# Split input-projection weights kept in DRAM between the two halves of the tokens

## The chip, the cores and the metric

The kernel runs on one core of a Trainium2 chip. Five engines work on their own instruction streams, each in order: TensorE (PE in the profile, PEld for its weight loads), VectorE (DVE), ScalarE (ACT), GpSimd (POOL) and SyncE (SP), which here only issues transfers. A transfer can be issued by SP, ACT or POOL. Engines wait for each other through semaphores. The metric is device time in microseconds (us) for one launch, less is better.

## The reference

One layer of a hybrid decoder over 2048 prompt tokens and 8 x 8 sample tokens, model width 1024. A combined input projection feeds a convolution branch and an RWKV-7 branch; an output projection with a residual and a final norm follow.

```python
xn = rms_norm(x, norm_g)
p = xn @ w_in                                   # 1024 -> 4224 columns
h, bg, cg, gc = conv columns, 512 each
u = cg * h;  z = causal width-3 convolution of u;  y_conv = bg * z * silu(gc)
pr = pr + mu_shift * (pr_prev - pr)             # token shift of the other 2176 columns
r, k, v, wl, al, gr = pr columns
S = S * w_t + (S @ -kk_t) (kk_t * a_t)^T + v_t k_t^T;  o_t = S r_t     # per head, 64 x 64
y_rwkv = (group_norm(o) + (r . k . r_k) v) * silu(gr)
y = x + concat(y_conv, y_rwkv) @ w_out;  return rms_norm(y), states
```

All of it is float32, and the products of the input projection have to be close to float32 in accuracy.

## The kernel before

The tokens are worked in two halves (`hf` 0 and 1) of 1024, the sample tokens with the first. A half is cut into three blocks of 256 or 330, 384 and 384 columns (`half_blocks`). The normalised inputs of a half lie transposed in SBUF as two parts, `xh` (rounded to the float32r type that TensorE multiplies) and `xl` (the rest), made by `xprep`.

`w_in` has 33 tiles of 128 output columns. `project` (line 297) takes one or two tiles: `load_w` (line 288) brings a tile's weights into SBUF and splits them in the same way, then per block 24 matmuls run, for each of the 8 slices of the contraction `wh*xh`, `wh*xl` and `wl*xh`, into one of two PSUM banks `pj`, and a function given by the caller empties the bank. The tile's weights are loaded and split in each half again, so 66 times in all.

`load_w` works in two pieces of 256 KB: SP issues the load into `wr` (two buffers), ACT copies it with rounding into `wh`, POOL subtracts to get `wl` (`split`, line 205; the copy is line 117, the subtraction line 207). `wh` and `wl` have two buffers each, so the weights of a tile are written when the tile two before it is done.

Two half times four pairs of heads make eight rounds (line 915, `s` = 0 to 7). A round projects k, r, then v and the gate together (`rwkv_pair`), and block by block computes decays, `bk` (lines 516 and 523), the A matrices (`amat`, POOL's `AB` at line 539) and sends diagonal blocks to DRAM (`dn`, line 622). `inverse` loads them back as `na` (line 634), runs a forward substitution on DVE (`subst`: the pairs `sub`, `xi`), sends the result out as `dx` and back into `AB` (line 663). `wkv` runs the recurrence in chunks of 64 tokens. `conv_group` projects the four convolution tiles h, C, B and G of the round, with sums on POOL (line 351) and DVE products that empty `pj` (shown as `hp` at line 123). In round 3 the convolution comes before the inverse, and `xprep(1)` follows it. After round 7 come the weights of the output projection and its 17 tiles.

The code is written stage after stage, but a planner sets the order of each engine's instructions from estimated durations, so that in the trace projections of the convolution run beside the substitution, and projections of the next round beside the recurrence. Buffers and waits are set by the same framework.

Of the kernel before, what the change touches and what calls it, by code (L numbers as in the profile page):

```python
# [8 lines left out]
F32 = mybir.dt.float32  # L9
# [6 lines left out]
DRAM = bass.MemoryType.DRAM  # L16
# [4 lines left out]
KT = D // 128  # L21
# [66 lines left out]
def trunk_kernel(ctx, tc, I, O):  # L88
    nc = tc.nc
    act, dve, pe, pool, sync = nc.scalar, nc.vector, nc.tensor, nc.gpsimd, nc.sync  # L90
# [5 lines left out]
    dram = ctx.enter_context(tc.tile_pool(name="dram", bufs=1, space=DRAM))  # L96
    cnt = [0]

    def T(pool, shape, tag, bufs=1, dt=F32):
        cnt[0] += 1  # L100
        return pools[pool].tile(shape, dt, tag=tag, bufs=bufs, name=f"{tag}_{cnt[0]}")
# [28 lines left out]

    yd = [[dram.tile([D, bl.nt], F32, name=f"yd{hf}{bl.i}") for bl in half_blocks(hf)] for hf in range(2)]

    # constants and parameters
    cst = T("const", [128, NCONST], "cst")
    warm = T("small", [128, 1], "ss", 2)
    pool.memset(warm, 0.0)
# [46 lines left out]
    for p in range(NPAIR):  # L183
        t = T("const", [128, 64], f"sst{p}")
# [1 line left out]
        sst.append(t)  # L186

    def rsqrt(x, n, rows=128, tag="x"):
        """x <- 1/sqrt(x) on [rows, n] of positive floats."""
        w = {"g": 6, "n": 3, "x": 1}[tag]  # L190
        nb = 2
        y = T("small", [128, w], "nwy" + tag, nb)[:rows, :n]
        a = T("small", [128, w], "nwa" + tag, nb)[:rows, :n]
        dve.tensor_scalar(out=a.bitcast(I32), in0=x.bitcast(I32), scalar1=1, scalar2=None,
                          op0=ALU.logical_shift_right)
        dve.tensor_scalar(out=y.bitcast(I32), in0=a.bitcast(I32), scalar1=-1.0, scalar2=MAGIC,
                          op0=ALU.mult, op1=ALU.add)
        for _ in range(3):
            mul(a, y, y)
            stt(a, a, -0.5, x)  # L200
            stt(y, a, 1.5, y, ALU.add, ALU.mult)
        return y

    # normalised inputs, transposed and split
    def split(hi, lo, src, eng=dve):
        copy(hi, src)
        eng.tensor_tensor(out=lo, in0=src, in1=hi.bitcast(F32), op=ALU.subtract)  # L207
# [77 lines left out]
                act.dma_start(out=O["shift_p"], in_=xts[-1][127:128, :])  # L285
        return xh, xl

    def load_w(src):
        wh = T("w", [128, KT, 128], "wh", 2, F32R)
        wl = T("w", [128, KT, 128], "wl", 2, F32R)  # L290
        for q in range(2):
            wr = T("w", [128, 4, 128], "wr", 2)
            sync.dma_start(out=wr, in_=src[:, q * 4:q * 4 + 4, :])
            split(wh[:, q * 4:q * 4 + 4, :], wl[:, q * 4:q * 4 + 4, :], wr, pool)
        return wh, wl

    def project(xs, hf, *tiles):
        ws = [load_w(I["w_in"][col // 128]) for col, _ in tiles]
        for bl in half_blocks(hf):
            for (wh, wl), (_, evac) in zip(ws, tiles):  # L300
                xh, xl = xs[0][bl.i], xs[1][bl.i]
                ps = PS([128, bl.cols], "pj", 2)
                for k in range(KT):
                    mm(ps, wh[:, k, :], xh[:, k, :], start=(k == 0), stop=False)
                    mm(ps, wh[:, k, :], xl[:, k, :], start=False, stop=False)
                    mm(ps, wl[:, k, :], xh[:, k, :], start=False, stop=(k == KT - 1))
                evac(bl, ps)
                yield
# [4 lines left out]
    def s8(ap):  # L313
        return ap[:, 0:64].rearrange("p (b j) -> p b j", j=8)

    # convolution branch
    def conv_group(xs, hf, g):
        sp = 80 if hf == 0 else 0
        u = T("half", [128, 1108], "hp", 4)
# [56 lines left out]
        yield from project(xs, hf, (CW + g * 128, ev_b))  # L376
        yield from project(xs, hf, (3 * CW + g * 128, ev_g))

    # token shift
    def shifter(hf, i, dst):  # L380
        state = {}

# [32 lines left out]
    def rwkv_pair(S, xs, la):  # L415
        hf, p = S.hf, S.p
# [4 lines left out]
        k = T("half", [128, 1108], "hp", 4)  # L421
        rr = T("half", [128, 1108], "hp", 4)
        ws = tmp()[:, 0:256]
# [16 lines left out]
        W = {}  # L440
# [9 lines left out]
            W[bl.i] = (wp, ws)  # L450

        def parts(bl):
            """(token slice, inner length, chunk slice, W view) of the sample and prompt parts of a block."""
            r = []
            e = 0
            if bl.samp:
                r.append((0, SAMP, slice(0, 1), W[bl.i][1], 8))
                e = 1
            r.append((bl.o, bl.np, slice(e, e + bl.nch), W[bl.i][0], 64))
            return r  # L460
# [136 lines left out]
        yield from vg  # L597

    def subst(na, x, n, par):
        """x[c, t] (columns c of the inverse, par of them per row step) by forward substitution."""  # L600
        rows = na.shape[0]
        cw = x.shape[1]
        for s in range(n - 1):
            w = min(s // par + 1, cw)
            m = n - 1 - s
            t = T("small", [128, 144], "sub", 1)[:rows, :w * m].rearrange("p (c t) -> p c t", t=m)
            mul(t, x[:, 0:w, s:s + 1].to_broadcast([rows, w, m]),
                na[:, s, s + 1:n].unsqueeze(1).to_broadcast([rows, w, m]))
            tt(x[:, 0:w, s + 1:n], x[:, 0:w, s + 1:n], t, ALU.add)
            if s % 4 == 3:  # L610
                yield

    def store_blocks(S, bl):
        """the diagonal 32 x 32 blocks to DRAM, one 64-token unit after the other."""
        if bl.i == 0:
            cnt[0] += 1
            S.dn = dram.tile([2, 2, 16, 32, 32], F32, tag="dn", bufs=2, name=f"dn_{cnt[0]}")
        e = 1 if bl.samp else 0
        for h in range(2):
            for b in range(2):  # L620
                r = h * 64 + b * 32
                sync.dma_start(out=S.dn[h, b, bl.ch0:bl.ch0 + bl.nch].rearrange("c s t -> s c t"),
                               in_=S.AB[bl.i][r:r + 32, e:e + bl.nch, b * 32:b * 32 + 32])
# [54 lines left out]
            copy(AB[0:32, e:e + n, 32:64], pt[0:32])  # L678
            dve.tensor_copy(out=AB[64:96, e:e + n, 32:64], in_=pt[64:96])

    # recurrence
    def group_tiles(S, bi, ca, n):
        """token-major beta/k (rows as in L) and v of up to four chunks of a block."""
        bt = T("ch", [128, 4, 128], "bt", 2)
        sv = T("ch", [128, 4, 2, 64], "sv", 2)
        pb = CX([128, 4, 128])
        for i in range(n):
            pe.transpose(out=pb[:, i, :], in_=S.bk[bi][:, ca + i].rearrange("p a t -> p (a t)"), identity=ident)  # L688
        copy(bt[:, 0:n, :], pb[:, 0:n, :])
        o = ca * 64  # L690
        if n == 1:
            pv = CX([64, 128])
            pe.transpose(out=pv, in_=S.v[bi][:, o:o + 64], identity=ident)
            copy(sv[64:128, 0, 0, :], pv[:, 0:64])
            copy(sv[0:64, 0, 1, :], pv[:, 64:128])
        else:
            m = n // 2
            pv = CX([128, m, 128])
            for i in range(m):
                pe.transpose(out=pv[:, i, :], in_=S.v[bi][:, o + i * 128:o + i * 128 + 128], identity=ident)  # L700
            svv = sv.rearrange("p (i r) h v -> p i r h v", r=2)
            for par in range(2):
                rows = slice(par * 64, par * 64 + 64)
                copy(svv[64:128, 0:m, par, 0, :], pv[rows, :, 0:64])
                copy(svv[0:64, 0:m, par, 1, :], pv[rows, :, 64:128])
        return bt, sv
# [115 lines left out]
        sync.dma_start(out=O["wkv_s"][p], in_=s0)  # L822

    def gn_out(S, ob, bl):
        """group norm, bonus and gate of a block."""
        e = 1 if bl.samp else 0
        n = bl.nch + e
        BV, SG = S.bv[bl.i], S.sg[bl.i]
# [35 lines left out]
        stt(yo, yo, pcol(P_LB, p), SG[:, :n * 64], ALU.add, ALU.mult)  # L864
        sync.dma_start(out=yd[S.hf][bl.i][CW + p * 128:CW + (p + 1) * 128, :], in_=yo)

    # output projection
    def out_weights():
        woh, wol = [], []
        for i, (a, n) in enumerate(((0, 2), (2, 3), (5, 3))):  # L870
# [44 lines left out]
    for s in range(8):  # L915
        hf, p = divmod(s, NPAIR)
# [43 lines left out]


def layout(inputs):
    """the arrays of the launch: the inputs, laid out with features on the partitions where the chip wants them."""
    import numpy as np

    def cols(name):
        return np.asarray(inputs[name]).reshape(-1, 128).T

    a = {n: np.asarray(inputs[n]) for n in inputs}
    r = {  # L970
        "consts": constants()[0],
        "masks": constants()[1],
        "params": np.concatenate([cols(n) for n in ("mu_shift", "k_k", "k_a", "r_k", "lnx_g", "lnx_b", "w0", "a0",
                                                    "conv_w")], axis=1),
        "w_da": np.concatenate([np.tile(a[n][0].reshape(64, NPAIR, 128).transpose(1, 0, 2), (1, 2, 1))
                                for n in ("w_dec2", "w_a2")], axis=2),
        "state_conv": a["state_conv"].reshape(NB * 2, 4, 128).transpose(2, 1, 0),
        "state_shift": a["state_shift"].reshape(NB, KT, 128).transpose(2, 1, 0),
        "state_wkv": a["state_wkv"].reshape(NB, NPAIR, 2, HD, HD).transpose(1, 2, 4, 0, 3).reshape(
            NPAIR, 128, NB, HD),  # L980
        "w_in": a["w_in"].reshape(KT, 128, -1, 128).transpose(2, 1, 0, 3),
        "w_out": a["w_out"][0],
        "norm_g": a["norm_g"],
        "final_norm_g": a["final_norm_g"],
        "x_prompt": a["x_prompt"][0],
        "x_sample": a["x_sample"].reshape(SAMP, D),
    }
    return {n: np.ascontiguousarray(v) for n, v in r.items()}
# [22 lines left out]
```

## Time and profile before

| | us |
|---|---|
| median of 3 runs | 1674.99 (1674.01 to 1675.52) |
| profiled execution: span from first to last instruction | 1669.8 |
| PE busy | 1548.2 (93%) |
| PEld busy | 1293.2 (77%) |
| DVE busy | 1046.6 (63%) |
| ACT busy | 652.7 (39%) |
| POOL busy | 338.2 (20%) |
| ACT's 132 copies into `wh` | 80.2 |

The page gives no other time of the profiled execution than its span. A busy share of an engine is an average over stages; PE's is that of a pipeline whose ends are modelled. A line of a group gives the engine, the operation, what it writes and reads, the number of instructions, the busy time, the mean of one in ns, and the idle time of the engine just before them with what ended it. In the timeline the number in brackets is that idle time and its releaser. Line 123 is the helper of most DVE operations, line 129 that of all matmuls, so one goes by the names of the tiles.

### The profile page before, as it was taken

The page shows a single profiled execution, that of the slowest core. Times are in us where ns is not written, and L with a number is a line of the kernel's source. Part 1 is how long each engine was busy: PE and PEld are TensorE (multiplying, and loading weights), DVE is VectorE, ACT ScalarE, POOL GpSimd, SP SyncE. Part 2 cuts the span into 40 slices and gives each one's busy share as a digit, 9 for nine tenths or more (in the row PEclk, how much of TensorE's full clock was granted, in tenths as well). Part 3 has the DMA queues.
Part 4 walks back from the last instruction along what each step waited for, and adds up shares of the span by engine and source line. Part 5 has one row for each costly group of instructions (what it writes and reads, how often), then busy time and mean ns, then how long its engine had stood idle before and what let it go on. Part 6 is the DMA issues. An engine that isn't in the chain of part 4 may idle for free.

```text
span 1669.8 us, 29362 instructions
## 1 busy us (share of the span) xinstructions
PE 1548.2 (93%) x11088; PEld 1293.2 (77%) x11088; DVE 1046.6 (63%) x3101; ACT 652.7 (39%) x1657; POOL 338.2 (20%) x395
## 2 busy tenths in 40 slices
PE   4989999989989999879988998899989999899997
PEld 4979778887778778867778778877887788567885
DVE  6377557765776469775577457745774577566554
ACT  5333345324532455254442454245424542342221
POOL 3233112421032103321033112311231123100000
PEclk9989999899989999989989998999899989799999
DMA  5101201120012102331012101210121023523441
GB/s 170 50 28 44 62 30 31 44 67 29 21 47 56 47 23 60 92 96 37 22 34 63 46 23 35 63 46 23 34 63 46 23 59 92 155 77 124 139 145 51
DMA packets 112463, 99.99 MB, mean 60 GB/s; under 512 B 61561, under 2 KB 85625, under 8 KB 112322
## 3 DMA queue, kind: packets, MB, share of 16 engines
q1 hardware_dynamic: 107024, 87.23, 18.0%
q10 hardware_dynamic: 5266, 10.86, 1.8%
q8 instruction: 88, 1.44, 0.4%
q14 instruction: 53, 0.43, 0.1%
q0 software_dynamic: 32, 0.03, 0.0%
HBM read 75.30 MB, written 22.75 MB: 59 GB/s over the span
## 4 chain that ended last, share of the span: by engine, by line
PE 64%; DVE 22%; DMA 5%; issue 4%; ACT 3%; SPq 1%; POOL 1%; POOLq 0%; ACTq 0%; DVEq 0%
PE pj L129 42%; PE ca L129 5%; PE ax L129 5%; DVE sub L123 5%; DVE xi L123 4%; PE cb L129 4%; PE oo L129 2%; DVE hp L123 2%; PE cx L129 2%; DMA na<-dn 2%; DVE bk L123 1%; DVE t L120 1%; PE cx L688 1%; DVE hp L120 1%; PE ax L282 1%
## 5 line engine op out<-in xcount | busy, mean ns | idle before, releaser
L129 PE MATMUL pj<-xh,wh 128*128 128x384 f32 (+3 forms) x1856 | 660.5, 356 | 31.8 <-DVE hp L123 30.4
L129 PE MATMUL pj<-xh,wl 128*128 128x384 f32 (+3 forms) x1856 | 658.8, 355 | 0.0
L129 PE MATMUL pj<-xl,wh 128*128 128x384 f32 (+3 forms) x1856 | 656.3, 354 | 2.6 <-POOL xl L207 2.2
L129 PEld LDWEIGHTS pj<-xh,wh 128*128 128x128 f32 x1856 | 360.3, 194 | 69.4 <-DVE hp L123 28.3
L129 PEld LDWEIGHTS pj<-xl,wh 128*128 128x128 f32 x1856 | 361.1, 195 | 30.2 <-POOL xl L207 3.0
L129 PEld LDWEIGHTS pj<-xh,wl 128*128 128x128 f32 x1856 | 360.2, 194 | 27.2 <-issue 2.7
L207 POOL TENSOR_TENSOR wl<-wr,wh 128x512 fp32r<-128x512 f32 x132 | 173.4, 1328 | 459.0 <-ACT wh L117 321.4
L117 ACT ACTIVATE wh<-wr 128x512 fp32r<-128x512 f32 x132 | 80.2, 625 | 162.9 <-PE pj L129 119.1
L117 ACT ACTIVATE tS<-sv,wc 64x64 f32<-64x64 f32 x256 | 88.0, 344 | 130.2 <-DVE sv L120 104.3
L129 PE MATMUL ax<-L,bk 64*128 64x128 f32 x528 | 89.5, 325 | 35.7 <-DVE bk L123 25.8
L129 PEld LDWEIGHTS ax<-L,bk 64*128 64x128 f32 x528 | 74.0, 219 | 54.2 <-POOL wl L207 26.7
L120 DVE SCALAR_TENSOR_TENSOR sv<-cb,wc,tS 64x64 f32<-64x64 f32 x240 | 67.9, 283 | 63.5 <-PE cb L129 52.2
L123 DVE TENSOR_TENSOR sub<-xi,na 128x126 f32<-128x126 f32 (+22 forms) x248 | 91.1, 367 | 17.3 <-DMA na<-dn 10.0
L117 ACT ACTIVATE t<-pj,prm 128x384 f32<-128x384 f32 (+3 forms) x170 | 68.8, 433 | 62.7 <-PE pj L129 59.5
L516 POOL TENSOR_TENSOR bk<-t,t 64x384 f32<-64x384 f32 (+2 forms) x56 | 56.2, 1003 | 173.8 <-ACT t L488 91.4
L736 DVE TENSOR_SCALAR u<-ca,Q 128x64 f32<-128x64 f32 x128 | 36.2, 283 | 85.7 <-PE ca L129 85.4
L123 DVE TENSOR_TENSOR xi<-xi,sub 128x126 f32<-128x126 f32 (+22 forms) x248 | 83.0, 335 | 7.3
L129 PEld LDWEIGHTS ca<-sv,L 128*64 128x64 f32 x528 | 43.4, 136 | 38.6 <-DVE sv L120 12.2
L726 DVE COPY xs<-ca 128x64 f32<-128x64 f32 x128 | 28.7, 225 | 68.7 <-PE ca L129 58.5
L129 PE MATMUL ca<-sv,L 128*64 128x64 f32 x528 | 68.4, 247 | 0.0
L123 DVE TENSOR_TENSOR AB<-ax,msk 64x384 f32<-64x384 f32 (+2 forms) x88 | 48.6, 553 | 28.9 <-PE ax L129 27.9
L123 DVE TENSOR_TENSOR hp<-pj,hp 128x512 f32<-128x512 f32 (+1 forms) x34 | 23.4, 689 | 62.6 <-PE pj L129 61.7
(201 smaller groups left out, 2027.1 us busy)
## 6 DMA issues: line engine op xcount, KB each, us to landing
wr<-in_w_in SPq DMA_DIRECT2D x132, 256.0 KB, 2.7
hp<-in_x_prompt SPq DMA_DIRECT2D x29, 512.0 KB, 3.7
la<-yd SPq DMA_DIRECT2D x16, 512.0 KB, 3.9
out_y_p<-hp ACTq DMA_DIRECT2D x16, 512.0 KB, 2.7
na<-dn SPq DMA_DIRECT2D x16, 256.0 KB, 4.0
hp<-in_w_out SPq DMA_DIRECT2D x8, 512.0 KB, 4.1
yd<-hp SPq DMA_DIRECT2D x16, 192.0 KB, 1.9
yd<-c SPq DMA_DIRECT2D x16, 192.0 KB, 1.9
```

The lines of the kernel that those rows point to most:

```text
L117: act.activation(out=out, in_=in_, func=AF.Copy, scale=scale, bias=bias)
L120: eng.scalar_tensor_tensor(out=out, in0=in0, scalar=scalar, in1=in1, op0=op0, op1=op1)
L123: dve.tensor_tensor(out=out, in0=in0, in1=in1, op=op)
L129: pe.matmul(out, lhsT=lhsT, rhs=rhs, start=start, stop=stop)
L207: eng.tensor_tensor(out=lo, in0=src, in1=hi.bitcast(F32), op=ALU.subtract)
L282: pe.transpose(out=ps[:, k, :], in_=xt[:, kk * 128:(kk + 1) * 128], identity=ident)
L516: pool.tensor_tensor(out=S.bk[bl.i][hs, chs, h, :], in0=ta[hs, a:a + n].rearrange("p (c j) -> p c j", j=64), in1=wi[hs, a:a + n].rearrange ...
L688: pe.transpose(out=pb[:, i, :], in_=S.bk[bi][:, ca + i].rearrange("p a t -> p (a t)"), identity=ident)
L726: dve.tensor_copy(out=xs_, in_=px)
L736: dve.tensor_scalar(out=u, in0=pu, scalar1=S.Q[:, q:q + 1], scalar2=None, op0=ALU.mult)
```

## The change

A DRAM tensor `wsp` holds for each of the 33 tiles both split parts. In the first half, after the split, SP stores `wh` and `wl` there, 512 KB each. In the second half neither `wr` nor the split is used: POOL issues two transfers from `wsp` straight into `wh` and `wl`. `project` tells `load_w` which tile and which half it is. `wsp` is of type float32; the stores read `wh` and `wl` as float32, the loads write them as float32r. The diff also drops some comments and docstrings, which moves line numbers by a few.

```diff
+    wsp = dram.tile([33, 2, 128, KT, 128], F32, name="wsp")
+
-    def load_w(src):
+    def load_w(src, col=None, hf=0):
         wh = T("w", [128, KT, 128], "wh", 2, F32R)
         wl = T("w", [128, KT, 128], "wl", 2, F32R)
+        if hf == 1:
+            pool.dma_start(out=wh, in_=wsp[col, 0])
+            pool.dma_start(out=wl, in_=wsp[col, 1])
+            return wh, wl
         for q in range(2):
             wr = T("w", [128, 4, 128], "wr", 2)
             sync.dma_start(out=wr, in_=src[:, q * 4:q * 4 + 4, :])
             split(wh[:, q * 4:q * 4 + 4, :], wl[:, q * 4:q * 4 + 4, :], wr, pool)
+        sync.dma_start(out=wsp[col, 0], in_=wh.bitcast(F32))
+        sync.dma_start(out=wsp[col, 1], in_=wl.bitcast(F32))
         return wh, wl

     def project(xs, hf, *tiles):
-        ws = [load_w(I["w_in"][col // 128]) for col, _ in tiles]
+        ws = [load_w(I["w_in"][col // 128], col // 128, hf) for col, _ in tiles]
```

## Prediction

> **What bounds the kernel now.** I read the chain of waits first, then PE's own waits in the stretch that changes most, then the timelines around its two largest stalls, then the clock there.
>
> ```profile
> span 1669.8 us, 29362 instructions
> ```
> ```profile
> PE 64%; DVE 22%; DMA 5%; issue 4%; ACT 3%; SPq 1%; POOL 1%; POOLq 0%; ACTq 0%; DVEq 0%
> ```
> ```profile
> L207 POOL TENSOR_TENSOR wl<-wr,wh 128x512 fp32r<-128x512 f32 x132 | 173.4, 1328 | 459.0 <-ACT wh L117 321.4
> ```
>
> PE and DVE carry 86% of the chain, and the split of the weights (ACT's copy, POOL's subtraction) hardly shows in it. So what the change takes off ACT and POOL is worth nothing by itself; it counts only where it held up DVE or PE. The second half of the tokens runs from about 850 to 1400 us (pairs 4 to 7). There PE itself waits for two things:
>
> ```profile
> PE pj L129 <- DVE hp L123: 13.7, 10, 3.3
> PE ax L129 <- DVE bk L123: 12.4, 9, 2.7
> ```
>
> Columns: us in total, times, longest. No weight is waited for. The first row is the projection of the convolution columns that finds both `pj` banks full, because DVE is late in emptying them; the second is the A matrices of a block waiting for DVE's `bk`. Why is DVE late?
>
> ```profile
> 1057.56 0.22 DVE L123 TENSOR_TENSOR xi<-xi,sub 128x58 f32<-128x58 f32 x1
> 1057.81 1.33 DVE L123 TENSOR_TENSOR sub<-xi,na 128x56 f32<-128x56 f32 x1
> ...
> 1070.32 1.27 DVE L123 TENSOR_TENSOR xi<-xi,sub 128x135 f32<-128x135 f32 x1
> 1071.62 1.26 DVE L123 TENSOR_TENSOR sub<-xi,na 128x126 f32<-128x126 f32 x1
> 1072.92 0.29 DVE L123 TENSOR_TENSOR xi<-xi,sub 128x126 f32<-128x126 f32 x1
> ```
> ```profile
> 1069.99 2.75 POOL L207 TENSOR_TENSOR wl<-wr,wh 128x512 fp32r<-128x512 f32 x2 [7.03 <-ACT wh L117]
> ```
> ```profile
> 1075.97 0.69 PE L129 MATMUL pj<-xh,wh 128*128 128x384 f32 x1 [3.27 <-DVE hp L123]
> ```
>
> The steps of the forward substitution take 0.2 to 0.3 us alone and about 1.3 us while POOL's two-input subtraction runs: each subtraction that falls on them costs DVE about 1 us, and 3.27 us later PE gets its bank. The second stall looks the same:
>
> ```profile
> 1018.53 1.36 DVE L123 TENSOR_TENSOR bk<-hp,t 64x384 f32<-64x384 f32 x1
> 1040.68 0.56 DVE L123 TENSOR_TENSOR bk<-hp,t 64x384 f32<-64x384 f32 x1
> ```
> ```profile
> 1018.22 2.80 POOL L207 TENSOR_TENSOR wl<-wr,wh 128x512 fp32r<-128x512 f32 x2 [0.56 <-ACT wh L117]
> ```
> ```profile
> 1020.04 0.34 PE L129 MATMUL ax<-L,bk 64*128 64x128 f32 x1 [2.62 <-DVE bk L123]
> ```
>
> Behind each stall TensorE loses clock. The windows view gives PEclk, the last column but two:
>
> ```profile
> 906.60:916.00 9.40, 6.16 (x26) 6.16 (x27) 7.68 (x31) 0.45 (x2) 0.01 (x1) 0.82 0.18 63
> 1072.70:1082.10 9.40, 6.13 (x19) 6.13 (x20) 7.72 (x31) 0.38 (x1) 0.04 (x1) 0.64 0.19 66
> 1240.00:1249.40 9.40, 6.08 (x19) 6.08 (x20) 7.77 (x31) 0.38 (x1) 0.09 (x1) 0.64 0.18 64
> ```
> ```profile
> 850.00:868.00 18.00, 14.73 (x65) 12.45 (x66) 12.54 (x21) 3.73 (x7) 5.91 (x7) 0.72 0.18 50
> ...
> 1352.00:1370.00 18.00, 15.06 (x55) 12.84 (x55) 11.19 (x21) 4.22 (x9) 3.94 (x5) 0.62 0.22 61
> ```
>
> Lost full-speed time is length times (1 - PEclk). After the bank stalls of pairs 4, 5 and 6: 1.7 + 3.4 + 3.4 = 8.5 us. After the `bk` stalls (the first and the last of four are shown; the two between are like the last): 5.0 + 3 x 6.8 = 25.4 us.
>
> **The change part by part.** *Second half, split removed.* 66 copies on ACT and 66 subtractions on POOL go (half of the 132). Per pair, three of the stretched substitution steps shown shrink by 1.33 - 0.22, 1.27 - 0.29 and 1.26 - 0.29, together 3.1 us, against a bank stall of about 4 us (13.7 less the last pair's share, over three pairs). I credit 3.1 x 3 = 9.3 us, and the 8.5 us of clock, since a stall under 1 us is left. At the `bk` stall the first `bk` shrinks from 1.36 to 0.56: 0.8 x 4 = 3.2 us. What is late next there is DVE's own row of operations ahead of it, and 1.8 us of stall stays; whether the clock survives 1.8 us is unknown, between 0 and 25.4 us, and I take 0, as the nearest row is a stall of 2.6 us, which it does not survive. Gain 21.0 us. The copies on ACT are costed at nothing: DVE's work hides them.
>
> *Second half, loads added.* Each weight tile now comes as two transfers of 512 KB that POOL issues when the tile's buffer comes free; until now a 256 KB piece lay in `wr` ahead of time, and only the split followed the release. No such load is in the trace. POOL's one transfer, 512 KB loads and a 512 KB store beside a small one:
>
> ```profile
> L272 POOL DMA_DIRECT2D out_shift_s<-hp x1: 728/728/728, 13.3 to 13.3; - x1
> ```
> ```profile
> hp<-in_x_prompt SPq DMA_DIRECT2D x29, 512.0 KB, 3.7
> ...
> out_y_p<-hp ACTq DMA_DIRECT2D x16, 512.0 KB, 2.7
> ...
> na<-in_x_prompt SPq DMA_DIRECT2D x1, 512.0 KB, 8.6
> ...
> dn<-AB SPq DMA_DIRECT2D x64, 24.0 KB, 1.6
> ```
>
> Issue costs POOL 0.73 us, 1.5 us per tile in place of 2.7. Landing lies between 3.7 us and the 8.6 us of one load that by the timeline stood behind two more of its size; I take 3.7, the median of 29 loads of this size. Where is there little time? Buffers alternate, so the tight hand-overs are v's to the convolution's h and r's to g:
>
> ```profile
> 1010.16 1.30 POOL L207 TENSOR_TENSOR wl<-wr,wh 128x512 fp32r<-128x512 f32 x1 [2.17 <-ACT wh L117]
> 1138.18 1.27 POOL L207 TENSOR_TENSOR wl<-wr,wh 128x512 fp32r<-128x512 f32 x1 [27.06 <-PE pj L129]
> ```
> ```profile
> 1014.53 0.28 PE L129 MATMUL pj<-xh,wl 128*128 128x256 f32 x1
> 1145.31 0.28 PE L129 MATMUL pj<-xh,wl 128*128 128x256 f32 x1
> ```
>
> The POOL rows start when `wl` is free, the PE rows are its first use: 4.4 us and 7.1 us. The first has 1.8 us more cover in the `bk` stall behind it, so 6.2 us. A 3.7 us landing fits both: cost 0; at 8.6 us it costs 2.4 + 1.5 = 3.9 us a pair, 15.6 in all. Behind a waiting issue on POOL stand `bk`, `AB` and the convolution's sums; but POOL stands at these releases already (the 321.4 us above, through ACT), so I count nothing for it.
>
> *First half, stores added.* 66 stores on SP, an issue of about 0.5 us each by the `wr` row below (1.01 for two), in a queue that is mostly idle. They read a buffer that is rewritten two projections later, hidden by a whole projection. What they can hold up is SP's small transfers, in front of the substitution:
>
> ```profile
> 141.88 1.76 SPq L622 DMA_DIRECT2D dn<-AB  x4
> 143.74 1.01 SPq L293 DMA_DIRECT2D wr<-in_w_in  x2
> 145.02 1.39 SPq L634 DMA_DIRECT2D na<-dn  x2
> ```
> ```profile
> 141.81 2.55 POOL L207 TENSOR_TENSOR wl<-wr,wh 128x512 fp32r<-128x512 f32 x2
> ```
>
> The stores become ready at 143 to 144.4 us, between `dn` and `na`. One 512 KB store in front costs 2.7 - 1.6 = 1.1 us by the store row, at most (8.6 - 3.7) / 2 = 2.45 by the queued load; two of them delay `na`, and with it DVE's whole chain, by 2.2 to 4.9 us. This falls on pairs 0, 1 and 2 (pair 3 projects its convolution before its inverse). I take 2.2 x 3 = 6.6 us, the row of a store.
>
> Sum: -21.0 + 6.6 = -14.4, a span of 1655.4 us. The median of the runs shown, 1674.99, is 5.2 above the profiled span; with that, **1661 us**.
>
> [...]
>
> **The rivals.** *A, the loads come late (slower).* Place: the two hand-overs. With landing X, the loss is 4 x ((X - 6.2) + (X - 7.1)); it eats the 14.4 us at X = 8.5, next to the 8.6 us row. At X = 12 the loss is 43 us: **1704**. For it: the destination is of another type than the DRAM tensor, and no such transfer is in the trace. Against: 8.6 us is one load, 3.7 the median of 29. [...]
>
> *B, POOL's issue holds DVE as the subtraction does (no change).* An issue is 0.73 us against 1.3, so 44% of the relief is left: 12.5 x 0.44 = 5.5 us, no clock regained, against 6.6 of stores: **1676**. The planner's new order of DVE could swallow as much; the interleaving of substitution and projections is its work, and I cannot see the new one.
>
> *C, the stores weigh more (slower).* 4.9 us and 3.4 us of clock per pair of the first half, 24.9, against 12.5 of relief without clock: **1687**.
>
> *D, the clock also survives the shorter `bk` stall (faster).* 25.4 us more: **1635**. [...]
>
> **How the numbers follow.** Forecast 0.42 (own range 1648 to 1671, the upper end with some of the landing's cost), D 0.15, B 0.17, C 0.13, A 0.13. A difference under 0.2% (3.3 us) cannot be told from none here. Faster: 0.42 + 0.15 = 0.57; same: B, 0.17; slower: A and C, 0.26. A range from 1630 to 1690 leaves out A and the tails, under 2 in 10.
>
> **What would show it.** Right: in the second half no DVE step of 1.3 us during the substitution, PE's wait for `hp` down from 13.7 to about 4 us, PEclk near 1 where it was 0.64. Wrong: PE waiting for the transfers into `wh` or `wl` (A), DVE still stretched beside POOL's issues (B), `na<-dn` landing later than its siblings of the second half and longer `hp` waits before 600 us (C).

## The result, and the profile after

The changed kernel takes 1631.20 us (median of 3 runs, 1630.60 to 1635.59) against 1674.99: a ratio of 0.974, 95% interval 0.972 to 0.977, so 43.8 us less. The direction was forecast, but the gain is three times the 14 us forecast; the time lies at the edge of the wide range (1630 to 1690) and below the forecast's own (1648 to 1671). The profiled span fell from 1669.8 to 1629.4 us.

From the page of the kernel after: span, chain by engine, and the two rows of POOL that the change touches.

```profile
span 1629.4 us, 29336 instructions
...
PE 64%; DVE 23%; DMA 5%; issue 3%; ACT 3%; SPq 1%; POOL 0%; ACTq 0%; DVEq 0%; POOLq 0%
...
L207 POOL TENSOR_TENSOR wl<-wr,wh 128x512 fp32r<-128x512 f32 x66 | 86.9, 1329 | 191.3 <-ACT wh L117 188.2
...
L294 POOL DMA_DIRECT2D wh<-wsp x33 | 18.7, 566 | 252.6 <-PE pj L129 177.4
```

The chain has the same mix as before; 66 of the 132 subtractions are gone. A page does not say where 40 us went; the windows do, cut at the same places of the work. First before, then after (start:end, length, then busy time of PE, PEld, DVE, ACT and POOL with instruction counts, PEclk, DMA share, GB/s):

```profile
0.00:848.50 848.50, 775.37 (x5716) 658.03 (x5717) 544.58 (x1604) 360.97 (x928) 195.92 (x246) 0.95 0.18 53
848.50:1400.50 552.00, 521.80 (x3918) 446.26 (x3916) 346.95 (x994) 215.61 (x554) 134.96 (x147) 0.94 0.16 46
1400.50:1669.80 269.30, 251.05 (x1456) 188.95 (x1456) 155.09 (x506) 76.07 (x176) 7.29 (x3) 0.96 0.35 111
```
```profile
0.00:843.00 843.00, 771.49 (x5723) 650.08 (x5723) 537.69 (x1607) 354.30 (x919) 188.95 (x247) 0.96 0.30 97
843.00:1364.00 521.00, 498.60 (x3914) 427.63 (x3914) 315.09 (x991) 184.90 (x497) 91.53 (x146) 0.97 0.26 77
1364.00:1629.40 265.40, 249.35 (x1456) 189.28 (x1455) 153.24 (x505) 76.21 (x176) 8.10 (x3) 0.96 0.36 113
```

The second half is 31.0 us shorter, the first 5.5, the tail 3.9. In the second half DVE is busy 31.9 us less (346.95 to 315.09). PE does nearly the same matmuls in 23.2 us less busy time (521.80 to 498.60) and stands idle 7.8 us less (552.00 - 521.80 = 30.2 before, 22.4 after). By PEclk, 552 x 0.06 = 33.1 us of full-speed time were lost before and 521 x 0.03 = 15.6 after, 17.5 us less. So over half of that gain is clock behind the stalls; the two ways of counting put it between 17.5 and 23.2 of the 31.0 us.

The 5.5 us of the first half are less than the runs differ among themselves: up to the first load of the second half (693.7 us) five of the kernels below (e3, e4, e6, e7, e9) are the same as the kernel after, and the first 4573 matmuls took 690.1 us in its profile and 687.4 to 696.5 in theirs. So this pair of profiles does not show that the first half gained.

PE's own waits in the second half after (total, times, longest), to set beside 13.7 and 12.4 us before:

```profile
PE cx L129 <- DVE na L673: 10.8, 3, 4.9
PE ax L129 <- DVE bk L123: 3.9, 8, 1.1
PE pj L129 <- DVE hp L123: 2.6, 3, 1.4
```

Both old waits have nearly gone and a new one has come: the inverse. PE has no projection left to do when `na` is made (line 673) from what comes back from DRAM, and DVE itself waits there for the transfer `AB<-dx` (8.7 us in three waits). Two things meet. PE is done with its projections earlier, and the inverse's transfers (`dx` out, `AB` back) land later beside the new loads. Their times from issue to landing in the second half, first before, then after:

```profile
DMA to landing us min/median/max: 1.6/1.9/3.5
```
```profile
DMA to landing us min/median/max: 1.6/3.5/6.3
```

In the longest of the three stalls (4.9 us) two loads are issued at 1060.61 us, between `dx` (1058.44) and `AB` (1062.75), and `na` follows `dx` by 11.1 us; in the same pair before it was 8.4. So 2.7 us of that stall are the later landing, and the rest is PE being done earlier. A run below bears this out: with the subtractions in quarters and no trip through DRAM (e14_before_quarters) the second half takes 527.5 us, nearly as little, these landings have a median of 1.9 us again, and PE waits 2.4 us for `na` in place of 10.8. Whether the loads and these transfers share a part of the DMA path is not shown.

The windows behind one of the old `bk` stalls, one of the old bank stalls, and the three new stalls, all after:

```profile
1005.00:1023.00 18.00, 16.95 (x104) 14.91 (x102) 15.09 (x31) 6.04 (x13) 4.18 (x8) 1.00 0.14 37
...
891.70:901.10 9.40, 8.02 (x47) 7.98 (x47) 7.37 (x28) 0.87 (x2) 0.00 (x0) 1.00 0.32 95
...
908.00:926.00 18.00, 18.00 (x202) 14.64 (x203) 4.56 (x13) 6.15 (x19) 0.73 (x1) 0.73 0.13 31
1070.00:1088.00 18.00, 18.00 (x223) 14.66 (x223) 5.22 (x15) 6.05 (x18) 1.10 (x2) 0.87 0.25 77
1226.00:1244.00 18.00, 17.84 (x189) 14.61 (x189) 4.20 (x12) 5.56 (x18) 0.72 (x1) 0.65 0.14 33
```

PEclk is 1.00 where it was 0.62 and 0.64. Behind the new stalls 18 x (0.27 + 0.13 + 0.35) = 13.5 us of clock are lost again. In the second half, stalls of 2.6 us already cost the clock before (0.62 to 0.72), and stalls of up to 1.4 us left it alone after (1.00). The length of one stall does not decide it, though. In the first half of the kernel after, the window behind a stall of 2.5 us (first line) kept its clock (1.00) and the one behind a stall of 1.5 us (second line) did not (0.61); what else decides is not shown here.

```profile
165.50:178.90 13.40, 10.64 (x60) 10.12 (x60) 8.44 (x32) 2.74 (x6) 1.89 (x4) 1.00 0.47 128
```
```profile
283.90:297.00 13.10, 11.56 (x42) 9.40 (x42) 8.98 (x20) 1.56 (x5) 3.73 (x6) 0.61 0.33 113
```

### The profile page after: what moved, and what is told of

It reads as the page before. It is cut to its first block, busy times and chain, and to the rows that moved or that the text cites. A ratio compares the mean times of both kernels' runs of the same rounds, so it can differ in the third digit from the quotient of the medians.

```text
span 1629.4 us, 29336 instructions
## 1 busy us (share of the span) xinstructions
PE 1519.4 (93%) x11088; PEld 1267.0 (78%) x11088; DVE 1006.0 (62%) x3101; ACT 615.4 (38%) x1591; POOL 288.6 (18%) x395
## 4 chain that ended last, share of the span: by engine, by line
PE 64%; DVE 23%; DMA 5%; issue 3%; ACT 3%; SPq 1%; POOL 0%; ACTq 0%; DVEq 0%; POOLq 0%
PE pj L129 42%; PE ca L129 5%; PE ax L129 5%; DVE xi L123 4%; DVE sub L123 4%; PE cb L129 4%; DVE hp L123 3%; PE oo L129 2%; PE cx L129 2%; DVE t L120 1%; DMA dx<-xi 1%; DVE bk L123 1%; PE cx L696 1%; DMA AB<-dx 1%; DVE hp L120 1%
## 5 line engine op out<-in xcount | busy, mean ns | idle before, releaser
L129 PE MATMUL pj<-xh,wl 128*128 128x384 f32 (+3 forms) x1856 | 651.3, 351 | 0.1
L129 PEld LDWEIGHTS pj<-xh,wl 128*128 128x128 f32 x1856 | 354.9, 191 | 27.4 <-issue 2.8
L207 POOL TENSOR_TENSOR wl<-wr,wh 128x512 fp32r<-128x512 f32 x66 | 86.9, 1329 | 191.3 <-ACT wh L117 188.2
L129 PE MATMUL ax<-L,bk 64*128 64x128 f32 x528 | 83.6, 309 | 22.1 <-DVE bk L123 14.9
L117 ACT ACTIVATE t<-pj,prm 128x384 f32<-128x384 f32 (+3 forms) x170 | 68.6, 433 | 68.3 <-PE pj L129 64.8
L123 DVE TENSOR_TENSOR sub<-xi,na 128x126 f32<-128x126 f32 (+22 forms) x248 | 76.2, 307 | 16.1 <-DMA na<-dn 8.9
L117 ACT ACTIVATE wh<-wr 128x512 fp32r<-128x512 f32 x66 | 40.5, 626 | 90.4 <-PE pj L129 79.2
L129 PEld LDWEIGHTS ca<-sv,L 128*64 128x64 f32 x528 | 43.0, 134 | 37.9 <-DVE sv L120 13.8
L294 POOL DMA_DIRECT2D wh<-wsp x33 | 18.7, 566 | 252.6 <-PE pj L129 177.4
L123 DVE TENSOR_TENSOR hp<-hp,pj 128x384 f32<-128x384 f32 (+2 forms) x56 | 25.6, 464 | 55.2 <-PE pj L129 55.0
```

The costliest lines, as they stand in the source:

```text
L117: act.activation(out=out, in_=in_, func=AF.Copy, scale=scale, bias=bias)
L123: dve.tensor_tensor(out=out, in0=in0, in1=in1, op=op)
L129: pe.matmul(out, lhsT=lhsT, rhs=rhs, start=start, stop=stop)
L294: pool.dma_start(out=wh, in_=wsp[col, 0])
```

## The experiments

The theory after the result: a DVE step that starts while POOL reads must sit out that whole POOL instruction; 1.3 us of subtraction makes DVE late, PE stalls, and the clock falls. The rivals: the planner's new order of the engines made the gain; ACT's freed copies made it; POOL's queue no longer stands in front of the sums that others need; the stores act in some way of their own. All ratios are against runs of the kernel before on the same chip in the same batch (medians 1673.2 to 1678.2).

| run | us | ratio to before (95%) |
|---|---|---|
| after | 1631.2 | 0.974 (0.972 to 0.977) |
| e1_stores_only | 1669.4 | 0.994 (0.990 to 0.998) |
| e2_loads_only | 1643.4 | 0.982 (0.978 to 0.985) |
| e3_pool_sub_back | 1667.6 | 0.996 (0.994 to 0.998) |
| e4_act_copy_back | 1630.6 | 0.973 (0.971 to 0.976) |
| e5_stores_tiny | 1673.1 | 0.999 (0.997 to 1.002) |
| e6_pool_memset | 1648.7 | 0.987 (0.983 to 0.991) |
| e7_pool_copy | 1648.9 | 0.985 (0.981 to 0.990) |
| e8_loads_twice | 1674.8 | 1.000 (0.997 to 1.002) |
| e9_fill_tied | 1631.5 | 0.972 (0.966 to 0.978) |
| e10_conv_dve | 1612.2 | 0.961 (0.956 to 0.966) |
| e12_pieces | 1611.9 | 0.961 (0.957 to 0.966) |
| e13_no_split | 1613.0 | 0.962 (0.958 to 0.967) |
| e14_before_quarters | 1633.3 | 0.973 (0.969 to 0.977) |
| e15_before_halves | 1643.2 | 0.982 (0.978 to 0.985) |
| e16_all_pieces | 1602.6 | 0.957 (0.953 to 0.960) |
| e17_after_all_pieces | 1591.6 | 0.950 (0.946 to 0.954) |

### The two halves of the change, each alone

Stores alone (against the kernel after):

```diff
-        if hf == 1:
-            pool.dma_start(out=wh, in_=wsp[col, 0])
-            pool.dma_start(out=wl, in_=wsp[col, 1])
-            return wh, wl
...
+        if hf == 0:
+            sync.dma_start(out=wsp[col, 0], in_=wh.bitcast(F32))
+            sync.dma_start(out=wsp[col, 1], in_=wl.bitcast(F32))
```

> The stores of the first half are kept, the second half splits its weights as before. My theory (relief of DVE in the second half, and TensorE's clock with it; the stores hidden): the first half keeps the 5.5 us that it gained in the profile of after, the second half gains nothing: 1675 - 5.5 = 1669 us (1665 to 1673). The prediction's step on the stores: 1675 + 6.6 = 1682 us. If the planner's new order made the gain in the first half alone, 1669 as well; on that the profile decides, since on every engine the first half stands in the order of after.

Loads alone, of the unsplit weights, with no stores (the kernel leaves the split of the second half out):

```diff
-            pool.dma_start(out=wh, in_=wsp[col, 0])
-            pool.dma_start(out=wl, in_=wsp[col, 1])
+            pool.dma_start(out=wh, in_=src)
+            pool.dma_start(out=wl, in_=src)
```

> No stores; the second half loads the unsplit weights into both tiles with the two transfers of 512 KB, so the split of the second half is left out of the computation. My theory: the second half and the tail gain what they gained in after, 43.8 - 5.5 = 38.3 us, the first half nothing: 1675 - 38.3 = 1637 us (1631 to 1643). If the stores themselves brought the gain (an order of SP that outlasts the first half), 1660 us or more.

Measured 1669.4 (6.3 less than before) and 1643.4 (32.2 less, 0.4 us above its range). They sum to 38.5 of the 43.8 us. With the stores alone PE's two waits in the second half stand where they stood before (13.8 and 12.2 us). The second half carries the gain, and the stores cost nothing that shows.

### Work put back into the second half, at the order of after

The subtraction again, into an unused tile; then ACT's copies again:

```diff
             pool.dma_start(out=wl, in_=wsp[col, 1])
+            for q in range(2):
+                wr = T("w", [128, 4, 128], "wr", 2)
+                qs = slice(q * 4, q * 4 + 4)
+                pool.tensor_tensor(out=wr, in0=wh[:, qs, :].bitcast(F32), in1=wl[:, qs, :].bitcast(F32), op=ALU.subtract)
```

> The kernel after, and in the second half POOL subtracts two 128x512 pieces per weight tile again, from wh and wl into an unused tile: 66 subtractions of 1.3 us that nobody waits for. PE, DVE, ACT and SP have the same order as in after. My theory (the subtraction stretches DVE's steps, PE's banks come late, the clock drops): DVE is stretched by about 20 to 27 us again, and with the clock the time rises by 15 to 31 us: 1646 to 1662 us. Rival, the planner's new order made the gain: 1631 us, within 3. Rival, the gain is that PE's first use of wl no longer waits for POOL: 1631 us, within 3.

```diff
+                copy(wr, wh[:, q * 4:q * 4 + 4, :].bitcast(F32))
```

> The kernel after, and in the second half ACT copies the two 128x512 pieces of each wh again, into an unused tile: 66 copies of 0.62 us that nobody waits for. My theory: ACT's copies stretch no DVE step and ACT is not on the path: 1631 to 1636 us. Rival, the gain came from ACT's freed time: 1645 us or more. The planner places some instructions of the second half anew here, so a few us either way mean nothing.

The subtractions that nobody reads cost 36.4 us (1667.6 against 1631.2), with every other engine in the order of after: above the range expected, and the rivals "order" and "PE's wait for `wl`" fall. Since the subtraction also stands in POOL's queue until its load lands, that rival is still open here. ACT's copies cost nothing (1630.6). The run with the subtraction: POOL's row, one pair of subtractions, the two DVE steps beside it, and PE's waits in the second half.

```profile
L299 POOL TENSOR_TENSOR wr<-wh,wl 128x512 f32<-128x512 f32 x66 | 86.0, 1319 | 80.3 <-DMA wl<-wsp 76.6 <-DMA dn<-AB 3.2
```
```profile
1065.63 2.55 POOL L299 TENSOR_TENSOR wr<-wh,wl 128x512 f32<-128x512 f32 x2 [1.36 <-DMA wl<-wsp]
```
```profile
1065.75 1.28 DVE L123 TENSOR_TENSOR sub<-xi,na 128x96 f32<-128x96 f32 x1
1067.07 1.23 DVE L123 TENSOR_TENSOR xi<-xi,sub 128x96 f32<-128x96 f32 x1
```
```profile
PE pj L129 <- DVE hp L123: 10.2, 6, 3.4
PE ax L129 <- DVE bk L123: 6.1, 10, 2.0
```

Steps that share nothing with these subtractions but the time take 1.23 to 1.28 us, and the bank wait is back at 10.2 us, from 2.6. The second half, cut at the same matmuls as in the kernel after (521.0 us, PEclk 0.97), takes 549.1 us, with the clock lower again:

```profile
854.30:1403.40 549.10, 510.56 (x3913) 435.81 (x3913) 339.10 (x987) 185.10 (x497) 163.51 (x202) 0.95 0.25 73
```

So by the profiles the subtraction alone takes back 28.1 of the second half's 31.0 us.

### What about POOL's work holds DVE?

In place of the subtraction: fills (write only), copies (one input), and fills tied to the load by a tiny copy on ACT, so that they wait where the subtraction waited:

```diff
+            wr = T("w", [128, 4, 128], "wr", 2)
+            for _ in range(5):
+                pool.memset(wr, 0.0)
```

> The kernel after, and in the second half POOL fills an unused tile five times per weight tile: 165 fills of 0.53 us that read nothing, the same 2.6 us of POOL per tile as the two subtractions. PE, DVE, ACT and SP have the order of after. Theory: what holds DVE is POOL's reading of two inputs, so fills cost nothing: 1627 to 1636 us. Rival, POOL's time itself (its queue, in which the sums for bk, AB and the convolution stand) or any work of POOL holds up the second half: 1655 us or more, as with the subtractions.

```diff
+                pool.tensor_copy(out=wr, in_=wh[:, q * 4:q * 4 + 4, :].bitcast(F32))
```

> The kernel after, and in the second half POOL copies the two 128x512 pieces of wh into an unused tile: 66 instructions with one input, each waiting for its load as the subtractions did, same order on the other engines. If it takes a second input on POOL to hold DVE: 1627 to 1636 us. If POOL's reading at all holds DVE's two-input steps, the cost goes by the time of the copy, unknown yet, between half and the whole of the subtraction's 36 us: 1649 to 1668 us. If waiting for the load in POOL's queue is what costs, as with the subtractions: 1660 us or more.

```diff
+            for q in range(2):
+                wr = T("w", [128, 4, 128], "wr", 2)
+                copy(wr[:, 0, 0:8], wh[:, q * 4, 0:8].bitcast(F32))
+                for _ in range(3 - q):
+                    pool.memset(wr, 0.0)
```

> The fills again, but tied to the landing of each weight tile by a copy of 8 columns on ACT, so that they stand in POOL's queue where the subtractions stood, beside the substitution: 165 fills of 0.53 us, same order on PE, DVE and SP. In the run before, the planner had put them in a heap at the change of halves, in front of the preparation of the second half's inputs. Theory (POOL's reading of two inputs holds DVE): 1627 to 1636 us. Rival (POOL's time, and its queue standing at the landing, delay the sums for bk, AB and the convolution): 1655 us or more, as the subtractions did (1667.6).

The tied fills cost nothing that shows: 1631.5 (1625.3 to 1641.2). They take POOL nearly as long as the subtractions (79.0 us against 86.0) and wait for the load nearly as long (64.8 against 80.3), so POOL's queue is not the cause. The run's POOL row, a group of fills, a DVE step beside it, and the second half cut at the same matmuls, as long as in the kernel after:

```profile
L300 POOL MEMSET wr<- 128x512 f32 x165 | 79.0, 524 | 64.8 <-ACT wr L117 64.6
```
```profile
1063.51 2.38 POOL L300 MEMSET wr<- 128x512 f32 x5 [2.77 <-ACT wr L117]
```
```profile
1063.77 0.27 DVE L123 TENSOR_TENSOR xi<-xi,sub 128x110 f32<-128x110 f32 x1
```
```profile
853.20:1374.70 521.50, 498.98 (x3914) 427.51 (x3914) 316.24 (x992) 192.78 (x551) 157.15 (x286) 0.97 0.26 77
```

The copies, half as long as the subtractions, cost 17.7 us (1648.9), at the lower end of the middle case, and their second half takes 533.1 us: one input on POOL is enough. A copy and the steps around it:

```profile
1057.69 0.61 POOL L298 COPY wr<-wh 128x512 f32<-128x512 f32 x1 [0.88 <-DMA wh<-wsp]
```
```profile
1057.50 0.24 DVE L123 TENSOR_TENSOR xi<-xi,sub 128x78 f32<-128x78 f32 x1
1057.77 0.64 DVE L123 TENSOR_TENSOR sub<-xi,na 128x100 f32<-128x100 f32 x1
```

So in these runs DVE's substitution steps of two inputs wait for POOL when it reads, about as long as that one instruction lasts (1.23 to 1.28 us beside subtractions of 1.3, 0.64 beside a copy of 0.61), and not when it only writes (0.27 beside the fills). Both sides show in the second half too: 549.1 us with the subtraction, 521.5 with the fills.

The untied fills missed their expectation, 1648.7. The planner had put them in a heap at the change of halves, and there a DVE operation on 128x3 elements took 8.22 us, beside 21 fills in a row, and ended with them (740.40 and 740.38 us); the same operation has a median of 0.17 us in the kernel after:

```profile
730.51 9.87 POOL L298 MEMSET wr<- 128x512 f32 x21
```
```profile
732.18 8.22 DVE L255 TENSOR_SCALAR ssx<-ssx 128x3 f32<-128x3 f32 x1 [0.60 <-ACT c L247]
```

This delays the inputs of the second half and says nothing of the substitution: the second half itself takes 520.3 us here, as in the kernel after, so the loss lies ahead of it.

### The stores, and the loads

The stores cut to 8 columns:

```diff
+            sync.dma_start(out=wsp[col, 0][:, 0:1, 0:8], in_=wh.bitcast(F32)[:, 0:1, 0:8])
+            sync.dma_start(out=wsp[col, 1][:, 0:1, 0:8], in_=wl.bitcast(F32)[:, 0:1, 0:8])
```

> The kernel with stores alone, each store cut to 8 of its 1024 columns, so that the instructions stay and the 34 MB do not move; the second half splits as before. The planner orders the first half in a third way. If the transfers themselves delay the substitution's small transfers (the prediction's step), this is faster than the run with whole stores by about 6.6 us: 1663 us or less. If the stores are hidden and the gain of the first half is a matter of the order in which the planner places its work, the difference to the run with whole stores (1669) is a few us of either sign, with TensorE's stalls at other places: 1664 to 1680 us.

Without the 34 MB the time is not lower but 3.8 us higher (1673.1 against 1669.4), with intervals that overlap at their edges. The transfers cost nothing that can be measured; what the stores alone gained (6.3 us) is left to the planner's order, by elimination and not by a run that holds it fixed.

Every load issued twice:

```diff
             pool.dma_start(out=wl, in_=wsp[col, 1])
+            pool.dma_start(out=wh, in_=wsp[col, 0])
+            pool.dma_start(out=wl, in_=wsp[col, 1])
```

> The kernel after, and every load of the second half is issued twice into the same tile, the second pair behind the first on POOL: twice the transfer, about 8 to 9.5 us to the landing. The planner's order of the second half changes with it. Rival A's formula, 4 x ((X - 6.2) + (X - 7.1)) with X = 9: 18.8 us more, 1650 us. My theory (in after PE waits for no load, the release of the buffers leaves more room than the two hand-overs of before showed): 1629 to 1640 us. If POOL's issue holds DVE (rival B), 66 more issues of 0.55 us: 1640 us or more, with DVE steps of over 1 us beside them.

Measured 1674.8, 43.6 us more than after: far from the theory's 1629 to 1640, the whole gain, and over double rival A's formula. With doubled loads, PE's waits from 835 to 1400 us, then POOL's row:

```profile
PE pj L129 <- DMA wl<-wsp: 9.3, 5, 3.5
...
PE pj L129 <- DVE hp L123: 8.2, 10, 1.6
...
PE pj L129 <- DMA wh<-wsp: 3.4, 2, 2.7
```
```profile
L296 POOL DMA_DIRECT2D wh<-wsp x33 | 18.0, 546 | 74.9 <-DMA wh<-wsp 70.2 <-ACT sv L117 4.5 <-issue 0.2
```

With doubled loads PE waits 12.7 us for them, and POOL stands 70.2 us at the first landing, with the sums behind it that DVE and PE need (`hp` from 2.6 to 8.2 us). In the kernel after neither PE nor its weight loads show a wait for a landing, but at one hand-over nothing is to spare. This load lands 5.3 us after its issue, at 1003.20 us, and its first matmul starts right then:

```profile
997.87 0.54 POOL L295 DMA_DIRECT2D wl<-wsp  x1
```
```profile
1003.24 0.39 PE L129 MATMUL pj<-xh,wl 128*128 128x256 f32 x1
```

Six small matmuls stood ahead of it (from 1002.35 us), so PE lost nothing that shows. The doubled loads also change the planner's order on PE, DVE and ACT; how the 43.6 us divide between the landings, POOL's queue, the clock and that order was not separated.

### The first half, and the length of one POOL instruction

On the kernel after: the first half's 32 convolution subtractions on DVE; all its subtractions in quarters; no split at all in either half:

```diff
-            split(wh[:, q * 4:q * 4 + 4, :], wl[:, q * 4:q * 4 + 4, :], wr, pool)
+            split(wh[:, q * 4:q * 4 + 4, :], wl[:, q * 4:q * 4 + 4, :], wr, dve if col < CONV_COLS // 128 else pool)
```

> The kernel after, with the subtractions of the first half's 16 convolution tiles on DVE in place of POOL (32 of 66). The profile of after shows a DVE operation of two inputs and 1024 columns at 1.2 us, so these are about 0.6 us each, 20 us of DVE in all; POOL's 66 stretch DVE by 29.6 us in the first half. If what is saved there outweighs it: 1615 to 1629 us. If DVE, which bounds these stretches, pays all of its own 20 us: 1633 to 1650 us.

```diff
-            split(wh[:, q * 4:q * 4 + 4, :], wl[:, q * 4:q * 4 + 4, :], wr, pool)
+            copy(wh[:, q * 4:q * 4 + 4, :], wr)
+            for k in range(4):
+                pool.tensor_tensor(out=wl[:, q * 4 + k, :], in0=wr[:, k, :], in1=wh[:, q * 4 + k, :].bitcast(F32), op=ALU.subtract)
```

> The kernel after, with each of the first half's subtractions on POOL cut into four of 128 columns, about 0.45 us each by the rows of POOL's small sums, same order on every engine. If DVE waits only for the POOL instruction at hand and then gets a step in between, a step loses 0.4 us in place of 1.0: 1615 to 1629 us. If DVE loses the whole time that POOL reads, now 1.8 us per piece of 512 in place of 1.33: 1632 to 1650 us.

```diff
-        if hf == 1:
...
+        pool.dma_start(out=wh, in_=src)
+        pool.dma_start(out=wl, in_=src)
         return wh, wl
```

> Both halves load the unsplit weights straight into both tiles by POOL; the split is left out of the computation in both. If the subtractions hurt the first half as they hurt the second (33 us there in the profiles): 1631 less 25 to 33, so 1598 to 1606 us. If the first half has other limits (start, the projections' own stalls): 1610 us or more.

All three land at 1612 to 1613, 18 to 19 us under after, the first two 3 us below their ranges. DVE's own subtraction (0.69 us each) is cheaper than POOL's of 1.33 beside it (1612.2 us against 1631.2), and quarters do as well as the run that leaves the split out; the symmetric 25 to 33 us that this last run was to bring did not come. Its planner's order is another one, and it brings loads into the first half, so it is no strict bound. The quarters run, POOL's row and DVE's steps beside the pieces:

```profile
L302 POOL TENSOR_TENSOR wl<-wr,wh 128x128 fp32r<-128x128 f32 x264 | 123.2, 500 | 181.5 <-ACT wh L117 178.4 <-PE pj L129 2.4 <-POOL xi L642 0.3
```
```profile
148.27 0.43 DVE L123 TENSOR_TENSOR sub<-xi,na 128x81 f32<-128x81 f32 x1
148.74 0.38 DVE L123 TENSOR_TENSOR xi<-xi,sub 128x81 f32<-128x81 f32 x1
```

Four quarters take POOL 2.0 us in place of 1.33, but DVE gets a step in after each: 0.4 us a step in place of 1.2 to 1.3. Then the same cut in the kernel before, in quarters and in halves, with every engine in the order of before; and with the products for `bk` and the convolution's sums in pieces of 128 columns too, on either kernel:

```diff
+            copy(wh[:, q * 4:q * 4 + 4, :], wr)
+            for k in range(0, 4, 1):
+                ks = slice(q * 4 + k, q * 4 + k + 1)
+                pool.tensor_tensor(out=wl[:, ks, :], in0=wr[:, k:k + 1, :], in1=wh[:, ks, :].bitcast(F32), op=ALU.subtract)
```

> The kernel before, no trip through DRAM, each of its 132 subtractions on POOL cut into four of 128 columns (about 0.45 us each, 1.8 us in place of 1.33 per 512 columns); every engine has the order of before. If the cost is the length of one POOL instruction that a DVE step sits out: both halves gain, 1605 to 1625 us, below the kernel after. If the trip through DRAM, its order or ACT's freed time is what gains: 1650 us or more. If DVE loses all the time in which POOL reads: 1675 us or more.

(With steps of 2 in place of 1:)

> The kernel before, each subtraction cut into two of 256 columns (about 0.75 us each), every engine in the order of before. If the cost grows with the length of one POOL instruction: between whole (1674) and quarters, 1630 to 1650 us. If only the sum of POOL's reading counts: 1674 us or more.

```diff
+                for x in range(0, n, 128):
+                    xs_ = slice(x, x + 128)
+                    pool.tensor_tensor(out=zp[:, xs_], in0=zp[:, xs_], in1=t[:, xs_], op=ALU.add)
...
+                    for x in range(0, n, 128):
+                        m = min(128, n - x)
+                        cs = slice(chs.start + x // 64, chs.start + (x + m) // 64)
+                        pool.tensor_tensor(out=S.bk[bl.i][hs, cs, h, :],
...
```

> The kernel before with its subtractions in quarters, and also POOL's products for bk (64x384, 1.27 us) and the convolution's sums (128x384, 1.02 us) in pieces of 128 columns; same order on PE, DVE, ACT and SP. In after these two still stretched DVE by about 42 us over both halves. If the rule holds for them: 5 to 20 us below the run with quarters alone. If their results are waited for, so that their own longer time counts: no gain, or up to 10 us more.

> The kernel after with the first half's subtractions, the products for bk and the convolution's sums in pieces of 128 columns, order of after on PE, DVE, ACT and SP. Against 1611.9 us with the subtractions alone in pieces: 5 to 15 us less if the rule holds for them, 1612 us or more if their own longer time is waited for. Against the run before it, which has no trip through DRAM: within 6 us if quarters make the split as good as free.

POOL's rows with halves and with quarters:

```profile
L297 POOL TENSOR_TENSOR wl<-wr,wh 128x256 fp32r<-128x256 f32 x264 | 201.7, 791 | 452.6 <-ACT wh L117 319.0 <-PE pj L129 125.8 <-DVE sub L123 2.9
```
```profile
L297 POOL TENSOR_TENSOR wl<-wr,wh 128x128 fp32r<-128x128 f32 x528 | 244.2, 496 | 433.0 <-ACT wh L117 304.1 <-PE pj L129 109.0 <-ACT bt L117 15.6
```

Whole, halves and quarters in the order of before: 1678.2 (the kernel before in that batch), 1643.2, 1633.3. POOL is busy longer each time (173.4, 201.7, 244.2 us) and the kernel gets faster, so it is the length of one instruction that costs. Quarters alone, with no trip through DRAM, equal the changed kernel (0.973 against 0.974); the 1605 to 1625 us expected of them did not come. The trip still adds to them: 1611.9 with both. The rule holds for the other sums too, and by more than the 5 to 20 and 5 to 15 us expected (30.7 and 20.3): 1602.6 without the trip, and **1591.6 with it, the best here, 40 us below the changed kernel and 0.950 (0.946 to 0.954) of the kernel before**. These two are 11 us apart where 6 at most was expected if quarters made the split as good as free. In the profiles, though, the second half, where only the first of them splits, takes 515.4 and 511.9 us; most of their distance lies in the first half, where both split, and its cause is open.

## Why the prediction was wrong in size

The gain came from the stretches as follows, by the profiled spans (us):

| stretch | forecast | measured |
|---|---|---|
| second half | -21.0 | -31.0 |
| first half (stores) | +6.6 | -5.5 |
| tail | 0 | -3.9 |
| sum | -14.4 | -40.4 |

So of the 26.0 us that the forecast missed, 10.0 lie in the second half, 12.1 in the first (where profiles of the same work differ by up to 9) and 3.9 in the tail, for which no row gives a cause. The mechanism, DVE held by POOL's subtraction, was right; two terms of the sum were not.

- **"I take 0" for the clock behind the `bk` stall: this is the step that failed in the second half.** The forecast chose the end of 0 to 25.4 us that belonged to a stall of 2.6 us, with 1.8 us left. The stall that was left is 1.1 us at most, PEclk behind it is 1.00, and the 25.4 us came.
- **Stores at 6.6 us: this is the step that failed in the first half.** The runs with stores alone are 6.3 us faster than before, with 0.998 as the upper end of the interval of the ratio; a cost of 6.6 us would be 1.004.
- **DVE's relief, 9.3 + 3.2 us of stalls:** the mechanism was right and shown by putting the subtraction back; the sizes were low. The bank wait fell by 11.1 us (13.7 to 2.6) and the `bk` wait by 8.5 (12.4 to 3.9). Counting three stretched steps per pair missed the others (DVE is busy 31.9 us less), and the first `bk` was not the only late step in its row.
- **What is late next** was named for the `bk` stall alone. The inverse, 10.8 us of wait and 13.5 us of clock in the second half, was not foreseen; without it the gain would have been larger still.
- **Rival D** had the right condition, at a chance of 0.15, but that its 1635 us lies so near 1631 is in part luck: for the second half it says 21.0 + 25.4 = 46.4 us where 31.0 came, and the first half and the tail, 16.0 us better than its sum has them, make up for it.
- **ACT's copies at nothing:** right (1630.6 with them back).
- **Loads at no cost:** right for the tiles that they bring, but only just (5.3 us from issue to use, above). Rival A had the right place; by its formula the loss starts at a landing of 6.2 us, and the median of `wl` is 4.7. The cost came where neither looked: the inverse's transfers land at a median of 3.5 us in place of 1.9, and PE waits behind them.

```profile
wh<-wsp POOLq DMA_DIRECT2D x33, 512.0 KB, 3.6
wl<-wsp POOLq DMA_DIRECT2D x33, 512.0 KB, 4.7
```

- **Rival B:** an issue takes POOL 0.57 us here, and DVE's steps beside one are untouched. An issue of the kernel after and the DVE step beside it:

```profile
1048.87 0.57 POOL L294 DMA_DIRECT2D wh<-wsp  x1 [7.35 <-PE pj L129]
```
```profile
1049.10 0.30 DVE L123 TENSOR_TENSOR sub<-xi,na 128x135 f32<-128x135 f32 x1
```

- **Where the stores' 6.6 us went:** the place was right, the size not. The two stores stand between `dn` and `na`, as forecast (SP's queue after), but `na` lands a median 4.1 us from its issue in place of 3.8 (first before, then after, the six of pairs 0 to 2):

```profile
137.09 1.75 SPq L630 DMA_DIRECT2D dn<-AB  x4
138.94 0.39 SPq L301 DMA_DIRECT2D wsp<-wh  x1
139.59 0.34 SPq L302 DMA_DIRECT2D wsp<-wl  x1
140.16 1.73 SPq L642 DMA_DIRECT2D na<-dn  x2
```
```profile
DMA to landing us min/median/max: 3.6/3.8/4.2
```
```profile
DMA to landing us min/median/max: 3.5/4.1/5.0
```

That is 0.3 us where 2.2 were taken, and `na` is issued no later behind `dn` than before (1.3 us after its last issue, 1.4 before): the step put the whole time of two stores in front of `na`, and most of it does not show there. Rival C falls with it. Why the stores alone are 6.3 us faster no row shows.

## What to carry to other kernels

Price a POOL instruction that reads SBUF by what one DVE step beside it must sit out (here about 1 us for a subtraction of 1.33), not by POOL's share of the span: cutting it into four cost POOL more here (244.2 us in place of 173.4) and gave as much as moving half of the split through DRAM (0.973 against 0.974). When a stall shrinks, price the clock behind it at both ends and ask what stall comes next; here the clock was 17.5 to 23.2 us of the second half's 31.0. And where a load is said to be hidden, look also at the small transfers that others wait for: this one was just hidden for its own tile at one hand-over (5.3 us from issue to use), while the inverse's landed at a median of 3.5 us in place of 1.9.

## What the runs showed of the hardware

- A POOL copy with one input, 0.61 us, holds a two-input DVE step as the subtraction does (0.64 us in place of about 0.25); fills of the same tile do not (0.27 us).
- A DVE TENSOR_SCALAR on 128x3 elements took 8.22 us while POOL ran 21 fills without a gap, and ended 0.02 us after the last of them; the same operation took a median of 0.17 us in the kernel after. Two-input steps beside quarter subtractions of 0.50 us took about 0.4 us each. What sets the two cases apart is not shown.
- In the second half, stalls of 2.6 us and more were followed by PEclk of 0.62 to 0.87, before and after, and those of at most 1.4 us in the kernel after by 1.00; in the first half of the kernel after one of 2.5 us was followed by 1.00 and one of 1.5 us by 0.61.
- In the second half of the kernel after, where POOL loads the weights in pieces of 512 KB, the inverse's transfers of 16 to 128 KB landed at a median of 3.5 us (at most 6.3); where SP loads them in pieces of 256 KB, at 1.9 (at most 3.5 in the kernel before, 5.0 in the run in quarters).
